# Two query tiles of an attention head handled together: one 256-column tile of probabilities, one 256-column product with the values

## The chip, the cores and the metric

The kernel runs on one core of one Trainium2 chip. The metric is the time of one execution on the device in microseconds (us): the median of 3 runs was 1680.57 us (1680.22 to 1680.72).

## The reference

Two layers work on 256 latent tokens and 256 context tokens of width 1024. Each layer is a feed-forward block, a mixer with attention heads of two kinds and a short convolution, and a second feed-forward block. In the last layer the context is only a source of keys and values. All values are float32.

```python
def gqa_attention(q, k, v):                     # heads A: 6 query heads, 2 key heads
    ...
    def block(qi):
        s = jnp.einsum('bqhgd,bkhd->bhgqk', qi, k).astype(jnp.float32) * scale
        p = jax.nn.softmax(s, axis=-1).astype(v.dtype)
        return jnp.einsum('bhgqk,bkhd->bqhgd', p, v)

def latent_mix(p, kv_ctx, cos, sin, qk_g, rpb, conv_w, rows):
    ...
    o_a = gqa_attention(qa, jnp.concatenate([ka, ka_c], axis=1), jnp.concatenate([va, va_c], axis=1))
    o_b = neighbourhood_attention(heads(qb, B_HEADS), kb, vb, kb_c, vb_c, rpb, rows)   # heads B, with a bias
    o_c = short_conv_mixer(cx, cb, cc, conv_w)
    return jnp.concatenate([o_a, o_b, o_c], axis=-1)
```

The queries and keys of heads A are normalised, multiplied by a gain (`qk_g`) and rotated; 1/8 is the scale of the scores. A latent query sees 512 keys (256 latent, 256 context), a context query sees the 256 context keys.

## The kernel before

Most products are of float32 numbers that are split into a high and a low part of type FP32R; three products (high by high, low by high, high by low) with moving operands of up to 512 columns are summed in PSUM by TensorE (`mm`, L88). `load_unit` (L95) loads a block of weights and splits it: ScalarE rounds the high part (L102), VectorE subtracts (L103).

`mixer` (L638) runs once for each layer. Tokens come in four tiles of 128 rows: 0 and 1 are latent, 2 and 3 are context. `token_block` (L656) makes V, queries and keys of heads A for a tile; it multiplies by the tile `GT` (L670), which the mixer builds first out of the gains `QK` with the factor 1/8 in it (L641 to L644). `fm_b` (L731) makes queries and keys of heads B, `fm_conv` (L756) the convolution.

`unit` (L785) handles one head and one tile of 128 queries: two products give the scores in a PSUM bank `at` (2 of them); VectorE finds the maximum (with the bias added, L796, or alone, L793); ScalarE takes the exponential with its sum (L801); VectorE divides (L803, L804); TensorE turns the probabilities over in blocks of 128 by 128 into a PSUM bank `ptr` (2 of them, L808); ScalarE copies them to an SBUF tile `PT` of up to 4 by 128 columns (L810; 3 such tiles in the first mixer, 4 in the second). Here P and PT are plain float32.

`pair` (L813) takes two heads and one query tile: two units, and then the values times the probabilities (L833 to L837) into one bank `pv`. Each of these products has 64 columns of V as its stationary operand and a block of PT as the moving one; the two heads alternate and write to partitions 0 to 63 and 64 to 127, that is, each uses one half of the array's columns. There are 4 products for 256 keys and 8 for 512 keys, and the profile shows two records for each product of plain float32. The result is copied out (L843) or, once the tiles `O` of the output projection are free, split into high and low part (`split_o`, L727).

```python
                for kb in range(nk // 128):
                    t = k0 // 128 + kb
                    for b in (1, 0):
                        vc = 64 * b if A else 128 + 64 * (2 * j + b)
                        mm(po[64 * b:64 * b + 64], V[:, t, vc:vc + 64], pts[b][:, kb], kb == 0, kb == nk // 128 - 1)
```

`attend` (L845) calls `pair` for three pairs of heads and the given query tiles: in the first mixer heads A and heads B for context and for latent queries (24 pairs), in the second one for latent queries alone (12 pairs). In the second mixer heads B of tile 0 come ahead of the convolution and those of tile 1 behind it. Behind all of this comes the output projection (L882 to L901), first all of tile 0, then all of tile 1 in the second mixer; each tile goes through `post` and `pre` (L218: a transposition at L215 and new columns of `Uh` and `Ul`) into the next feed-forward block, whose first products (`up_first`, L599) read these columns.

The order in which each engine issues its instructions is not the order of the code: a scheduler puts it together ahead of time from the code order as priority, the dependences and its own durations; the products of L837 have a raised priority. On the chip each engine then keeps to that order.

Of the kernel before, what the change touches and what calls it, by code (L numbers as in the profile page):

```python
# [25 lines left out]
def tile_hybrid_block(ctx: ExitStack, tc: tile.TileContext, xin, c2, crow, w_ada, w_ada0, bcol, gcol, win, qkg, bias_in,  # L26
# [468 lines left out]
    def ffn(ph, l, i, U, tiles, after, ada_target, mode, first=None):  # L495
# [27 lines left out]
        def up_out(fs, pss, c0, n):  # L523
            for f in fs:
# [9 lines left out]
                if f == 10:  # L534
                    n0 = len(nc.cur_bb.bb.instructions)
                    G.append(load_gate(l, mi, 1 if len(tiles) == 2 else 2))
                    if mode == "k":
                        pool.dma_start(out=ROPE, in_=rope)
                        pool.dma_start(out=CW, in_=convw)
                        pool.dma_start(out=QK.rearrange("p a d -> p (a d)"),  # L540
                                       in_=bass.AP(tensor=qkg.tensor, offset=qkg.offset, ap=[[0, 128], [1, 256]]))
                    for late in nc.cur_bb.bb.instructions[n0:]:
                        tc.add_manual_dep(late, ins.ins.name,
                                          mybir.DependencyInfo(mybir.DependencyClass.NoSync,
                                                               mybir.DependencyReason.DATA), reason="late load")
# [92 lines left out]
    def mixer(ph, l, U, after):  # L638
        full = l == 0
        order = (2, 3, 0, 1)  # L640
        GT = ph.tile([128, 8, 64], F32, name="GT", tag="GT")  # L641
        for h0, nh, row, sc in ((0, 6, 2 * l, 0.125), (6, 2, 2 * l + 1, 1.0)):
            dve.tensor_scalar(out=GT[:, h0:h0 + nh], in0=QK[:, row].unsqueeze(1).to_broadcast([128, nh, 64]),
                              scalar1=sc, scalar2=None, op0=ALU.mult)  # L644
# [11 lines left out]
        def token_block(t):  # L656
# [13 lines left out]
            dve.tensor_tensor(out=qn[:, h0:8], in0=qn[:, h0:8], in1=GT[:, h0:8], op=ALU.mult)  # L670
# [114 lines left out]
        def unit(q, k, kl, nk, bias):  # L785
# [23 lines left out]
            PT = ph.tile([128, 4, 128], F32, name="PT", tag="PT", bufs=3 if full else 4)  # L809
            act.copy(PT[:, 0:nb], pt[:, 0:nb])  # L810
            return PT

        def pair(A, j, qt):  # L813
            lat = qt < 2
            k0, nk = (0, 512) if lat else (256, 256)
            pts = []
            for b in range(2):
                qs = slice(128 * qt, 128 * qt + 128)
                ks = slice(k0, k0 + nk)
                if A:  # L820
                    pts.append(unit(AQ[:, j, b, qs], AK[:, b, ks], AL[:, b, ks], nk, None))
                else:
                    bias = None
                    if lat:
                        h = 2 * j + b
                        bias = BIAS[bn[0] % len(BIAS)]
                        bn[0] += 1
                        (sp).dma_start(out=bias[:, 0:256], in_=bias_in[l, h, qt])
                    pts.append(unit(BQ[j][b][:, qs], BK[j][b][:, ks], BL[j][b][:, ks], nk, bias))
            pb = bank("pv")  # L830
            po = pb[:, 0:128]
# [7 lines left out]
            qs = slice(128 * qt, 128 * qt + 128)  # L839
# [5 lines left out]
        def attend(A, qts):  # L845
            for j in range(3):
                for qt in qts:
                    pair(A, j, qt)

        def convert(c0, mks, n=256):  # L850
            c = slice(c0, c0 + n)
            for mk in mks:
                split_o((slice(None), mk, c), of(mk, c))
# [3 lines left out]
        if full:  # L857
            attend(True, (2, 3))
# [3 lines left out]
        attend(True, (0, 1))  # L862
        if full:
            attend(False, (2, 3))
# [3 lines left out]
            attend(False, (0, 1))  # L868
            convert(0, (0, 1, 2, 6, 7))
        else:  # L870
            attend(False, (0,))
            fm_conv()
            O.extend(new_u())
            convert(0, (0, 1, 2, 6, 7))
            convert(0, (3, 4, 5), 128)
            attend(False, (1,))
# [135 lines left out]
```

## Time and profile before

| | |
|---|---|
| median of 3 runs | 1680.57 us (1680.22 to 1680.72) |
| profiled execution | 1680.1 us, of which the traced span is 1678.2 us |
| TensorE matmul (PE) busy | 1665.8 us, 99% of the span |
| TensorE weight load (PEld) busy | 1399.2 us, 83% |
| VectorE (DVE) busy | 1134.2 us, 68% |
| ScalarE (ACT) busy | 717.5 us, 43% |
| GpSimd (POOL) busy | 47.0 us, 3% |
| granted TensorE clock, mean over the span | 0.999 of 2.4 GHz |

The first mixer runs from about 395 to 620 us of the span, the second from about 1340 to 1500 us. PE and PEld are the two halves of TensorE: a weight load can lie beside a matmul. The duration of a matmul's record is longer than the distance to the next one, since matmuls are pipelined: the time that a matmul costs is read from the distance of starts.

### The profile page before, as it was taken

What the parts mean: (1) busy time and instruction counts of PE and PEld (TensorE: products, weight loads), DVE (VectorE), ACT (ScalarE), POOL (GpSimd) and SP (SyncE); (2) the same over time, 40 slices, a digit from 0 to 9 for tenths busy, and PEclk for the clock granted to TensorE, in tenths of its full rate; (3) what the DMA queues carried; (4) which work ended last, traced back from release to release, by engine and by line L of the source; (5) the groups of instructions that cost most, each with busy time, mean ns of one, the idle gap of its engine ahead of it and who ended that gap; (6) DMA issues with size and microseconds to landing.
All of it is one profiled execution on the core that took longest, in us unless ns stands there. A gap on an engine that the chain in (4) does not pass through costs nothing.

```text
span 1678.2 us, 22858 instructions
## 1 busy us (share of the span) xinstructions
PE 1665.8 (99%) x8792; PEld 1399.2 (83%) x8792; DVE 1134.2 (68%) x1899; ACT 717.5 (43%) x1240; POOL 47.0 (3%) x77
## 2 busy tenths in 40 slices
PE   9999999999999999999999999999999999999998
PEld 7888888888877798888888888888888889879997
DVE  4578788667776665476675566787785668865554
ACT  5442222236566683322222364322223557865442
POOL 0000000001000010000000000000000010000000
PEclk9999999999999999999999999999999999999999
DMA  8476565433121234454444144665464222446552
GB/s 325 172 249 221 166 196 202 156 107 107 63 76 51 95 128 163 149 199 141 161 164 150 52 151 163 214 203 188 164 223 151 76 101 101 138 168 222 176 191 73
DMA packets 73501, 259.95 MB, mean 155 GB/s; under 512 B 8440, under 2 KB 11728, under 8 KB 72496
## 3 DMA queue, kind: packets, MB, share of 16 engines
q1 hardware_dynamic: 72144, 252.81, 44.4%
q0 software_dynamic: 1248, 5.68, 0.9%
q8 instruction: 69, 1.13, 0.3%
q14 instruction: 40, 0.33, 0.1%
HBM read 257.37 MB, written 1.09 MB: 154 GB/s over the span
## 4 chain that ended last, share of the span: by engine, by line
PE 98%; issue 1%; ACT 1%; DMA 0%; DVE 0%; SPq 0%; DVEq 0%; POOLq 0%; POOL 0%; ACTq 0%
PE mm L88 53%; PE at L88 27%; PE pv L88 14%; PE ptr L808 2%; PE ptr L215 1%; PE ptr L88 1%; DMA H<-in_xin_dram 0%; PE ptr L687 0%; PE ptr L611 0%; ACT uf L229 0%; ACT Uh L322 0%; ACT junk L198 0%; DVE w L340 0%; ACT w L336 0%; ACT w L102 0%
## 5 line engine op out<-in xcount | busy, mean ns | idle before, releaser
L88 PE MATMUL mm<-Uh,w 128*128 128x512 f32 (+1 forms) x1712 | 478.6, 358 | 0.8 <-DVE w L340 0.8
L102 ACT CAST w<-stg 128x1024 fp32r<-128x1024 f32 x254 | 266.5, 1050 | 403.6 <-PE mm L88 362.8
L103 DVE TENSOR_TENSOR w<-stg,w 128x1024 fp32r<-128x1024 f32 x254 | 310.1, 1222 | 146.1 <-ACT w L102 145.7
L88 PEld LDWEIGHTS mm<-Uh,w 128*128 128x128 f32 x1712 | 305.5, 189 | 46.8 <-DVE w L340 1.3
L152 DVE CUSTOM_DVE_ANT_0 uf<-adas,CB 128x1024 f32<-128x1024 f32 x248 | 302.9, 1221 | 18.2 <-DMA adas<-in_w_ada_dram 14.4
L88 PE MATMUL mm<-Ul,w 128*128 128x512 f32 (+1 forms) x856 | 305.9, 357 | 0.0
L88 PE MATMUL at<-Uh,w 128*128 128x512 f32 (+1 forms) x912 | 256.6, 359 | 0.1
L88 PE MATMUL mm<-w,a 128*128 128x512 f32 x924 | 223.9, 390 | 0.0
L88 PEld LDWEIGHTS mm<-w,a 128*128 128x128 f32 x924 | 172.9, 188 | 35.7
L88 PEld LDWEIGHTS at<-Uh,w 128*128 128x128 f32 x912 | 163.1, 189 | 26.6 <-issue 1.2
L88 PEld LDWEIGHTS mm<-Ul,w 128*128 128x128 f32 x856 | 161.7, 189 | 23.1
L88 PE MATMUL mm<-w,Uh 128*128 128x512 f32 (+1 forms) x544 | 170.5, 387 | 0.4 <-ACT w L102 0.4
L88 PE MATMUL at<-Ul,w 128*128 128x512 f32 (+1 forms) x456 | 163.3, 358 | 0.0
L88 PE MATMUL at<-w,a 128*128 128x512 f32 x570 | 137.3, 389 | 0.0
L88 PEld LDWEIGHTS at<-w,a 128*128 128x128 f32 x570 | 106.7, 188 | 21.9
L88 PE MATMUL pv<-Uh,w 128*128 128x512 f32 (+1 forms) x416 | 118.3, 361 | 0.3 <-DVE w L340 0.3
L88 PEld LDWEIGHTS mm<-w,Uh 128*128 128x128 f32 x544 | 100.1, 188 | 19.5 <-ACT w L102 0.7
L527 DVE TENSOR_TENSOR sg<-mm,sg 128x512 f32<-128x512 f32 (+1 forms) x80 | 50.4, 630 | 90.7 <-PE mm L88 85.1
L103 DVE TENSOR_TENSOR w<-stgx,w 128x1024 fp32r<-128x1024 f32 x58 | 71.0, 1224 | 52.6 <-ACT w L102 52.4
L88 PE MATMUL mm<-w,Ul 128*128 128x512 f32 (+1 forms) x272 | 105.1, 386 | 0.0
L88 PEld LDWEIGHTS at<-Ul,w 128*128 128x128 f32 x456 | 86.2, 189 | 12.9 <-DVE Ul L325 0.4
L526 ACT ACTIVATE sg<-at 128x512 f32<-128x512 f32 (+1 forms) x55 | 30.1, 547 | 152.6 <-PE at L88 146.1
(188 smaller groups left out, 1770.2 us busy)
## 6 DMA issues: line engine op xcount, KB each, us to landing
adas<-in_w_ada_dram SPq DMA_DIRECT2D x144, 512.0 KB, 3.7
stg<-in_wi_dram SPq DMA_DIRECT2D x122, 512.0 KB, 4.2
stg<-in_wo_dram SPq DMA_DIRECT2D x66, 512.0 KB, 3.3
stg<-in_win_dram SPq DMA_DIRECT2D x40, 512.0 KB, 3.2
stgx<-in_wi_dram SPq DMA_DIRECT2D x38, 512.0 KB, 4.3
stgx<-in_wo_dram SPq DMA_DIRECT2D x22, 512.0 KB, 4.3
stg<-in_woa_dram SPq DMA_DIRECT2D x16, 512.0 KB, 3.2
stg<-in_wi_tm_dram SPq DMA_DIRECT2D x16, 512.0 KB, 3.2
```

The costliest lines, as they stand in the source:

```text
L88: pe.matmul(out, lhsT=lhsT, rhs=rhs, start=first, stop=last)
L102: act.copy(w[:, 0], s)
L103: dve.tensor_tensor(out=w[:, 1], in0=s, in1=w[:, 0].bitcast(F32), op=ALU.subtract)
L152: dve.tensor_tensor_reduce(out=junk, in0=s, in1=CB[:, v], op0=ALU.mult, op1=ALU.add, scale=1.0, scalar=0.0, accum_out=ada_mc[m][:, v, cb:c ...
L215: pe.transpose(pt[:, b], xn[:, 128 * k:128 * k + 128], I)
L526: act.activation(sg[:, 0:n], pss[f, 0][:, 0:n], AF.Silu)
L527: dve.tensor_tensor(out=sg[:, 0:n], in0=pss[f, 1][:, 0:n], in1=sg[:, 0:n], op=ALU.mult)
L808: pe.transpose(pt[:, b], P[:, 128 * b:128 * b + 128], I)
```

## The change

Probabilities of both query tiles of a head go into one tile PT of 4 by 256 columns, each unit filling its 128 columns; `pair` now takes two heads and two query tiles (four units, head 1 first), and each product with the values moves 256 columns. PT has 2 buffers in both mixers. In the second mixer the convolution moves behind the first pair of heads B, and both query tiles of the other two pairs come behind it. Beside this, `GT` is gone: 1/8 is multiplied into `QK` once, behind its load in the first feed-forward block, and the product with the gains becomes two instructions (queries, keys).

```diff
                         pool.dma_start(out=QK.rearrange("p a d -> p (a d)"),
                                        in_=bass.AP(tensor=qkg.tensor, offset=qkg.offset, ap=[[0, 128], [1, 256]]))
+                        qk = QK.rearrange("p (l a) d -> p l a d", a=2)[:, :, 0]
+                        dve.tensor_scalar(out=qk, in0=qk, scalar1=0.125, scalar2=None, op0=ALU.mult)
...
-        GT = ph.tile([128, 8, 64], F32, name="GT", tag="GT")
-        for h0, nh, row, sc in ((0, 6, 2 * l, 0.125), (6, 2, 2 * l + 1, 1.0)):
-            dve.tensor_scalar(out=GT[:, h0:h0 + nh], in0=QK[:, row].unsqueeze(1).to_broadcast([128, nh, 64]),
-                              scalar1=sc, scalar2=None, op0=ALU.mult)
...
-            dve.tensor_tensor(out=qn[:, h0:8], in0=qn[:, h0:8], in1=GT[:, h0:8], op=ALU.mult)
+            for ha, hb, row in ((h0, 6, 2 * l), (6, 8, 2 * l + 1)):
+                if ha < hb:
+                    dve.tensor_tensor(out=qn[:, ha:hb], in0=qn[:, ha:hb],
+                                      in1=QK[:, row].unsqueeze(1).to_broadcast([128, hb - ha, 64]), op=ALU.mult)
...
-        def unit(q, k, kl, nk, bias):
+        def unit(q, k, kl, nk, bias, PT, c):
...
-            PT = ph.tile([128, 4, 128], F32, name="PT", tag="PT", bufs=3 if full else 4)
-            act.copy(PT[:, 0:nb], pt[:, 0:nb])
-            return PT
-
-        def pair(A, j, qt):
-            lat = qt < 2
+            act.copy(PT[:, 0:nb, c:c + 128], pt[:, 0:nb])
+
+        def pair(A, j, q0):
+            lat = q0 == 0
             k0, nk = (0, 512) if lat else (256, 256)
...
+            pts = [None, None]
+            for b in (1, 0):
+                pts[b] = ph.tile([128, 4, 256], F32, name="PT", tag="PT", bufs=2)
+                for qi in range(2):
+                    qt = q0 + qi
+                    qs = slice(128 * qt, 128 * qt + 128)
+                    if A:
+                        unit(AQ[:, j, b, qs], AK[:, b, ks], AL[:, b, ks], nk, None, pts[b], 128 * qi)
...
             pb = bank("pv")
-            po = pb[:, 0:128]
+            po = pb[:, 0:256]
...
-            qs = slice(128 * qt, 128 * qt + 128)
+            qs = slice(128 * q0, 128 * q0 + 256)
...
-            attend(False, (0,))
+            attend(False, 0, (0,))
             fm_conv()
             O.extend(new_u())
-            convert(0, (0, 1, 2, 6, 7))
-            convert(0, (3, 4, 5), 128)
-            attend(False, (1,))
+            convert(0, (0, 1, 2, 3, 6, 7))
+            attend(False, 0, (1, 2))
```

The scheduler's order moves with it. **TensorE, second mixer, the last two pairs of heads.** `pv<-PT,V` are the products with the values (64 columns of V by 128 or 256 columns of PT), `ptr<-I,P` the turned probabilities, `mm<-w,Uh` and `mm<-w,Ul` the output projection. Before:

```order
L88 MATMUL pv<-PT,V 64x128 x8
L808 MATMUL ptr<-I,P 128x128 x4
L88 MATMUL mm<-w,Uh 128x512
L88 MATMUL mm<-w,Ul 128x512
L88 MATMUL mm<-w,Uh 128x512 x2
L88 MATMUL mm<-w,Ul 128x512
L88 MATMUL mm<-w,Uh 128x512 x2
L88 MATMUL mm<-w,Ul 128x512
L88 MATMUL mm<-w,Uh 128x512 x2
L88 MATMUL mm<-w,Ul 128x512
L88 MATMUL mm<-w,Uh 128x512 x3
L88 MATMUL pv<-PT,V 64x128 x8
```

And with the change:

```order
L88 MATMUL pv<-PT,V 64x256 x7
L809 MATMUL ptr<-I,P 128x128 x8
L88 MATMUL mm<-w,Uh 128x512 x3
L809 MATMUL ptr<-I,P 128x128 x4
L88 MATMUL pv<-PT,V 64x256
L88 MATMUL mm<-w,Ul 128x512
L88 MATMUL mm<-w,Uh 128x512
L88 MATMUL mm<-w,Ul 128x512
L88 MATMUL mm<-w,Uh 128x512
L88 MATMUL mm<-w,Ul 128x512
```

Before, the products of a pair stood together, 4 or 8 in a row, in all 36 pairs. Now the first product (head 1, first key block) stands alone as soon as the tile of head 1 is whole, and the other 3 or 7 follow later, behind other work; this is so in all 18 pairs.

**TensorE, second mixer, behind the last product with the values.** `ptr<-I,xn` is the transposition of token tile 0 (L215), `at<-w,Uh` the first product of the next feed-forward block that reads the new columns of tile 0. Before:

```order
L88 MATMUL pv<-PT,V 64x128 x8
L88 MATMUL mm<-w,Ul 128x512
L88 MATMUL mm<-w,Uh 128x512
L88 MATMUL mm<-w,Ul 128x512
L88 MATMUL mm<-w,Uh 128x512
L215 MATMUL ptr<-I,xn 128x128 x8
L88 MATMUL mm<-w,Uh 128x512 x2
L88 MATMUL mm<-w,Ul 128x512
L88 MATMUL mm<-w,Uh 128x512 x2
```

And with the change:

```order
L88 MATMUL mm<-w,Uh 128x512 x2
L88 MATMUL mm<-w,Ul 128x512
L88 MATMUL mm<-w,Uh 128x512
L215 MATMUL ptr<-I,xn 128x128 x8
L88 MATMUL at<-w,Uh 128x512
L88 MATMUL mm<-w,Uh 128x512
L88 MATMUL at<-w,Ul 128x512
```

Before, 18 products of the output projection of tile 1 stood between that transposition and the first `at<-w,Uh`; now there are none. Behind the last product with the values stand 51 products of the output projection in place of 22.

**VectorE, first feed-forward block, the new product on `QK`** (L543 is the added line):

```order
L103 TENSOR_TENSOR w<-stg,w 128x1024
L543 TENSOR_SCALAR QK<-QK 128x2x64
L152 ISA uf,mc<-adas,CB 128x1024
L152 ISA mc 128x1
L527 TENSOR_TENSOR sg<-mm,sg 128x512
```

Before, the same rows stood without L543.

## Rows read from the trace of the kernel before

**Rows 1.** The page, part 4: the chain that ended last, share of the span by engine.
```profile
PE 98%; issue 1%; ACT 1%; DMA 0%; DVE 0%; SPq 0%; DVEq 0%; POOLq 0%; POOL 0%; ACTq 0%
```

**Rows 2.** Windows, mixers: from:to, length, busy PE, PEld, DVE, ACT, POOL; clock; DMA.
```profile
395.00:620.00 225.00, 224.09 (x1328) 182.72 (x1328) 156.62 (x363) 145.49 (x339) 14.49 (x18) 1.00 0.24 81
536.00:560.00 24.00, 23.52 (x177) 17.80 (x176) 19.11 (x66) 18.42 (x59) 0.00 (x0) 1.00 0.24 78
1340.00:1500.00 160.00, 158.74 (x1021) 134.32 (x1021) 121.94 (x270) 113.90 (x234) 11.02 (x17) 1.00 0.35 120
```

**Rows 3.** Tile V: all products with the values (ns min/median/max, first and last start).
```profile
L88 PE MATMUL pv<-PT,V x480: 272/273/324, 450.8 to 1476.1; 128*64 128x128 f32 x160
```

**Rows 4.** Timeline of PE round one block (start us, us, engine, line, what, count).
```profile
450.46 0.40 PE L88 MATMUL mm<-Ul,w 128*128 128x512 f32 x1
450.79 0.66 PE L88 MATMUL pv<-PT,V 128*64 128x128 f32 x8
451.38 0.44 PE L808 MATMUL ptr<-I,P 128*128 128x128 f32 x2
```

**Rows 5.** Timeline of PE round a block of 512 keys, second mixer.
```profile
1439.66 0.40 PE L88 MATMUL mm<-w,Uh 128*128 128x512 f32 x1
1439.98 1.09 PE L88 MATMUL pv<-PT,V 128*64 128x128 f32 x16
1441.01 0.96 PE L88 MATMUL at<-w 128*128 128x512 f32 x3
```

**Rows 6.** The chain in order of time: start us, us, what.
```profile
64.40 5.44 PE at L88 x24
```

**Rows 7.** Groups by line and form, 8 to 600 us: xcount | busy us, mean ns.
```profile
L88 PE MATMUL ptr<-adas,S 128*32 128x128 f32 x256 | 8.6, 276 | 0.0
L88 PE MATMUL at<-AL,AQ 128*128 128x512 f32 x12 | 4.7, 393 | 0.0
L88 PE MATMUL at<-AL,AQ 128*128 128x256 f32 x12 | 3.5, 288 | 0.0
```

**Rows 8.** Tile ptr, 49 to 57 us: float32 products of 4 columns (ns min/median/max).
```profile
L88 PE MATMUL ptr<-SELM,R x4: 168/210/253, 50.9 to 56.5; 128*128 128x4 f32 x4
```

**Rows 9.** Groups of weight loads by form, whole span.
```profile
L88 PEld LDWEIGHTS pv<-PT,V 128*64 128x64 f32 x480 | 25.5, 136 | 10.9 <-issue 5.5 <-ACT P L801 2.0 <-ACT PT L810 1.1
L88 PEld LDWEIGHTS ptr<-adas,S 128*32 128x32 f32 x256 | 6.5, 109 | 2.4 <-issue 2.1
```

**Rows 10.** Timeline, second mixer's end: token tile 0 into the next block.
```profile
1477.29 1.04 PE L215 MATMUL ptr<-I,xn 128*128 128x128 f32 x8
...
1478.08 0.70 PE L88 MATMUL mm<-w,Uh 128*128 128x512 f32 x2
...
1479.81 1.05 ACT L102 CAST w<-stg 128x1024 fp32r<-128x1024 f32 x1
...
1480.76 0.62 ACT L233 CAST Uh<-uf 128x512 fp32r<-128x512 f32 x1
...
1482.29 0.39 PE L88 MATMUL at<-w,Uh 128*128 128x512 f32 x1
```

**Rows 11.** Timeline of PE: token tile 1 into the next block.
```profile
1495.55 0.50 PE L88 MATMUL at<-w,Uh 128*128 128x512 f32 x1 [1.11 <-ACT Uh L233]
```

**Rows 12.** Groups by form, first mixer: copies of turned probabilities out of PSUM.
```profile
L810 ACT COPY PT<-ptr 128x512 f32<-128x512 f32 x24 | 13.7, 587 | 7.8 <-PE ptr L808 7.8
```

**Rows 13.** Tile GT: its four instructions and its readers (ns min/median/max).
```profile
L670 DVE TENSOR_TENSOR qn<-qn,GT x8: 286/684/693, 409.0 to 1384.4; 128x512 f32<-128x512 f32 x6, 128x128 f32<-128x128 f32 x2
L643 DVE TENSOR_SCALAR GT<-QK x4: 217/287/352, 402.7 to 1349.3; 128x384 f32<-128x384 f32 x2, 128x128 f32<-128x128 f32 x2
```

**Rows 14.** Tile QK: its load.
```profile
L540 POOL DMA_DIRECT2D QK<-in_qkg_dram x1: 536/536/536, 122.2 to 122.2; - x1
...
DMA to landing us min/median/max: 8.1/8.1/8.1
```

**Rows 15.** Timeline of DVE, first feed-forward block.
```profile
137.66 1.22 DVE L103 TENSOR_TENSOR w<-stg,w 128x1024 fp32r<-128x1024 f32 x1
```

More of the change, by code (lines that the diff above doesn't have):

```diff
@@ L808, in unit @@
                 pe.transpose(pt[:, b], P[:, 128 * b:128 * b + 128], I)
-            PT = ph.tile([128, 4, 128], F32, name="PT", tag="PT", bufs=3 if full else 4)
-            act.copy(PT[:, 0:nb], pt[:, 0:nb])
-            return PT
-        def pair(A, j, qt):
-            lat = qt < 2
-            k0, nk = (0, 512) if lat else (256, 256)
-            pts = []
-            for b in range(2):
-                qs = slice(128 * qt, 128 * qt + 128)
[L819 to L829, printed above, removed]
+            act.copy(PT[:, 0:nb, c:c + 128], pt[:, 0:nb])
+        def pair(A, j, q0):
+            lat = q0 == 0
+            k0, nk = (0, 512) if lat else (256, 256)
+            ks = slice(k0, k0 + nk)
+            pts = [None, None]
[6 more added lines that the diff above has]
+                        unit(AQ[:, j, b, qs], AK[:, b, ks], AL[:, b, ks], nk, None, pts[b], 128 * qi)
+                    else:
+                        bias = None
+                        if lat:
+                            h = 2 * j + b
+                            bias = BIAS[bn[0] % len(BIAS)]
+                            bn[0] += 1
+                            (sp).dma_start(out=bias[:, 0:256], in_=bias_in[l, h, qt])
+                        unit(BQ[j][b][:, qs], BK[j][b][:, ks], BL[j][b][:, ks], nk, bias, pts[b], 128 * qi)
             pb = bank("pv")
-            po = pb[:, 0:128]
+            po = pb[:, 0:256]
             with tc.high_priority():
@@ L838, in pair @@
             mk = j if A else 3 + j
-            qs = slice(128 * qt, 128 * qt + 128)
+            qs = slice(128 * q0, 128 * q0 + 256)
             if O:
@@ L843, in pair, with attend @@
                 act.copy(of(mk, qs), po)
[L845 to L848, printed above, removed]
+        def attend(A, q0, js=(0, 1, 2)):
+            for j in js:
+                pair(A, j, q0)
         def convert(c0, mks, n=256):
@@ L857, in mixer @@
         if full:
-            attend(True, (2, 3))
+            attend(True, 2)
         for t in (0, 1):
@@ L861, in mixer @@
         fm_b()
-        attend(True, (0, 1))
+        attend(True, 0)
         if full:
-            attend(False, (2, 3))
+            attend(False, 2)
             fm_conv()
@@ L867, in mixer @@
             convert(256, range(8))
-            attend(False, (0, 1))
+            attend(False, 0)
             convert(0, (0, 1, 2, 6, 7))
         else:
-            attend(False, (0,))
+            attend(False, 0, (0,))
             fm_conv()
             O.extend(new_u())
-            convert(0, (0, 1, 2, 6, 7))
-            convert(0, (3, 4, 5), 128)
-            attend(False, (1,))
+            convert(0, (0, 1, 2, 3, 6, 7))
+            attend(False, 0, (1, 2))
             act.activation(work.tile([128, 1024], BF16, name="junk", tag="junk")[:, 0:1], last_sm[0], AF.Silu)
```

## The prediction

> **What bounds the kernel now.** I read the chain that ended last first: 98% of the span is TensorE [rows 1]. Then the busy time by stretch: in the first mixer TensorE is busy for 224.09 of 225 us, in the second for 158.74 of 160, while VectorE and ScalarE are busy for some 65 to 76% [rows 2]. So inside the mixers too the kernel costs what TensorE's instructions cost, and a microsecond more or less there is one in the end. The granted clock is at its upper level (2.4 GHz) in both stretches, and nothing in the change empties TensorE for long; I leave the clock alone. What the other engines do counts only where TensorE comes to wait.
>
> **The products with the values, before.** There are 480 records with 128 moving columns [rows 3]: 12 pairs with 256 keys (8 records each) and 24 with 512 keys (16 records). What a block costs I read from starts. A product of 512 columns comes every 0.227 us (24 in 5.44 us) [rows 6]. In the first example the last such product starts at 450.46, so the next one could start at 450.69; behind the block of 8 TensorE starts on something else at 451.38 [rows 4]: 0.69 us. With 512 keys: 1439.66 plus 0.23 is 1439.89, then 1441.01 [rows 5]: 1.12 us for 16 records. The 8 records more cost 0.43 us. The two heads use different halves of the columns and go side by side, so this is four steps of two records, 0.108 us a step; and 0.69 less four steps leaves **0.26 us that a block costs whatever its length**, in front of it and behind it. All of it: 12 x 0.69 + 24 x 1.12 = 35.2 us.
>
> **The same, with the change.** First the step of 256 columns, which no row shows. A float32 record of 4 columns takes 168 ns at the least [rows 8], one of 128 columns 272 [rows 3]: 0.84 ns a column. FP32R records go from 288 to 393 ns between 256 and 512 columns [rows 7]: 0.41 ns a column. So float32 pays by the column, at twice the rate of FP32R, and 128 columns at 0.84 ns are 0.107 us, which is the whole step. I take 2 x 0.108 = 0.216 us. Bounds: below, 0.108 (columns free), above, 0.227, the step of an FP32R record of twice as many columns. Moving 256 columns at once then saves nothing by itself: half the steps at twice the price. What could be saved is the 0.26 us of each block: 36 blocks would become 18, 4.7 us.
>
> But the new order does not keep the blocks whole. In all 18 pairs the first product stands alone and the other 3 or 7 stand further on. That keeps 36 blocks, so the 4.7 us are not saved. And the lone product uses half the array: its two records cost 2 x 0.216 = 0.43 us with nobody beside them. In the rest head 0 has one product more than head 1 (2 to 1 or 4 to 3), so it takes as many steps as the whole block would have taken: 4 or 8. Sum: 18 x (0.43 + 0.26) + 6 x (4 x 0.216 + 0.26) + 12 x (8 x 0.216 + 0.26) = 12.4 + 6.7 + 23.9 = 43.0 us. **The values cost 7.8 us more than before**, which is 18 x 0.43.
>
> **What of it lies beside waiting.** TensorE's idle time in the mixers is 0.9 and 1.3 us [rows 2]; 0.48 of it lies in 536 to 560 us, where heads B of the context run with the least other work. There longer products fill gaps: -0.5 us. Bounds: 0 and -1.1 (that, and half of the rest). The other 1.1 us of the second mixer is one wait, next.
>
> **The end of the second mixer.** Before, tile 0 of the tokens was through its attention early; between its transposition and the first product on its new columns stood 18 products, and nothing waited long. Now both tiles end together, and no product stands there. From the first other instruction behind the transposition (1478.08) to the end of the rounding of the first half of the new columns (1480.76 + 0.62 = 1481.38) are 3.3 us [rows 10], with one rounding of weights of 1.05 us between. Without it, 2.25 us. I take 2.8 us of new waiting, bounds 2.25 and 4.2 (until 1482.29, when the first product did start). Against that, tile 1 before waited 1.11 us for its columns [rows 11]; now 20 products (4.5 us) stand in front of that product, longer than the 3.3 us, and the wait goes. Together +1.7 us, bounds +1.1 and +3.1.
>
> **At no cost.** `GT` goes (4 instructions of 0.22 to 0.35 us), and the product with the gains splits: two instructions of at most 0.69 and 0.29 us for one of 0.69 [rows 13], at most 6 x 0.29 us more on VectorE, which is busy for 157 of 225 us in the first mixer and has TensorE's other products as cover; without that cover, 0.3 us for each of four latent or context tiles. The new product on `QK` needs its load, landed at 122.2 + 8.1 = 130.3 us [rows 14]; it stands behind a weight split that starts at 137.66 [rows 15], so it waits for nothing and delays VectorE by some 0.2 us. Copies of results become half as many and twice as wide: ScalarE gains a little that nobody waits for. SP issues the same loads in nearly the same order; POOL's order is unchanged.
>
> **The new dependence.** Two PT tiles serve four units, so the first copy of a pair waits for the last product of the pair before. Only two `ptr` banks hold turned probabilities meanwhile, so the third transposition waits for that copy: 0.59 us [rows 12], against 0.40 us of the second transposition in front of it (half of the 0.79 us between 1477.29 and 1478.08 for eight blocks [rows 10]). If nothing else stands between, that is 0.19 us a pair, and with the way of the signals I put 0.3 us (an estimate): 5.4 us in all. The order puts other products between in most places; I take 0 and keep 5.4 as the bound.
>
> **Sum.** 7.8 - 0.5 + 1.7 = +9.0 us on the profiled execution's 1680.1: **1689.1 us**. The median of the runs is 0.5 us above that execution, less than any term here.
>
> **The rivals.**
> *Columns are nearly free* (faster). If the step of a record is set by its weight load and not by its columns, 256 columns also cost 0.108 us. Steps: 240 before; now 18 x 2 + 6 x 4 + 12 x 8 = 156. That is 84 x 0.108 = 9.1 us less, and 1680.1 - 9.1 - 0.5 + 1.7 = 1672.2 us. It decides from a step under 0.166 us on (240 x 0.108 / 156). For it: each record here has a load of its own, of 136 ns [rows 9], longer than the step. Against it: float32 records with loads of 32 columns (109 ns) [rows 9] take 276 ns [rows 7], those with 64 columns 273 [rows 3]: the shorter load buys nothing; and the record of 4 columns is short. The Trainium skill speaks for this rival, in the page "TensorE: Matmul & The Clock Gate", section "Back-to-back issue gap": sustained, about 81 ns at 128 columns and 131 ns at 512, far less than in proportion. By that ratio a step of 256 columns would be about 1.2 times one of 128 (an estimate from that page), and the sum would come to about 1676 us. The trace does not agree: 512 columns come every 227 ns here.
>
> *Lone products without the fixed part* (no change to slightly slower). The 0.26 us was read from blocks with both halves at work. If a lone product slips in without it, 18 x 0.26 = 4.7 us are off: 1684.4 us, and with the bounds of the two waiting terms (-1.1, +1.1) 1683.2. For it: no row shows a lone block. Against it: the part in front and behind looks the same for 8 and 16 records.
>
> *PT starves TensorE* (slower still): the bound above, 1689.1 + 5.4 = 1694.5 us. For it: in 536 to 560 us ScalarE is busy for 18.42 of 24 us, VectorE for 19.11 [rows 2]. Against it: the scheduler knows of the two tiles and has put products in between.
>
> **How the numbers follow.** Forecast 0.62, lone products without the fixed part 0.14, starving 0.16, columns nearly free 0.08. A measurement can tell 0.2%, 3.4 us, from no change: under 1677.2 is faster, over 1683.9 slower. The forecast with its bounds (1687.9 from 7.8 - 1.1 + 1.1, 1691.0 from 7.8 + 0 + 3.1, and 1692.8 with steps of 0.227, which make the 7.8 into 9.6) is slower; the second rival falls on both sides of 1683.9, and I give it to "same"; the first is faster. Faster 0.08, same 0.14, slower 0.78. The range of 8 in 10 is 1683 to 1695: it leaves out the fast rival, the least of the second one and what lies beyond starving.
>
> **What would show it.** Right: 240 records of 128*64 by 256 columns at about 0.216 us from start to start, each lone pair of them with some 0.7 us between its neighbours; TensorE still busy for nearly the whole of both mixers, which are longer by 7 to 8 us together before the end of the second one; a wait of TensorE of 2 to 3 us for the new columns of tile 0 behind the transposition at L215. Wrong: records of 256 columns that follow at under 0.17 us; lone products with no gap round them; or waits of TensorE for copies to PT, which would be listed under its waits in the mixers.

## The result and the profile after

The changed kernel takes **1697.97 us** (median of 4 runs, 1697.57 to 1698.64) against 1680.52 for the kernel before: a ratio of 1.0104, 95% interval 1.0092 to 1.0116. That is 17.4 us slower. The direction was forecast; the size, +9.0 us, was not, and the time lies above the range of 1683 to 1695. The profiled execution has a span of 1695.6 us, 17.4 longer than before, so the traces can be compared term by term.

The page of after, part 4, the chain that ended last, by engine (before: [rows 1]):

```profile
PE 96%; ACT 1%; DVE 1%; DMA 1%; issue 1%; SPq 0%; POOL 0%; DVEq 0%; POOLq 0%; ACTq 0%
```

Windows of after; columns as in [rows 2]. The first mixer is nearly as full as it was (1.62 us idle of 225, before 0.91). The second one, which is longer, has 7.17 us idle of 180, where before it was 1.26 of 160. Three quarters of that (3.54 and 1.82) lie in the last two windows, and there the granted clock is no longer 1.00:

```profile
395.00:620.00 225.00, 223.38 (x1133) 173.30 (x1132) 151.83 (x354) 140.15 (x316) 14.49 (x17) 1.00 0.22 76
1340.00:1520.00 180.00, 172.83 (x970) 140.75 (x969) 128.90 (x279) 119.82 (x238) 11.55 (x18) 0.98 0.34 116
...
1492.00:1497.00 5.00, 1.46 (x10) 0.86 (x8) 3.30 (x8) 4.88 (x11) 0.53 (x1) 0.94 0.50 159
1497.00:1503.20 6.20, 4.38 (x10) 3.01 (x11) 5.61 (x8) 4.76 (x9) 1.11 (x3) 0.50 0.73 262
```

Tile V of after, the products with the values (ns min/median/max, first and last start; before: [rows 3]):

```profile
L88 PE MATMUL pv<-PT,V x240: 379/379/431, 450.7 to 1479.7; 128*64 128x256 f32 x120
```

There are half as many records, and they are 106 ns longer (median). Timeline of PE of after, a lone product and a whole block of 7 in the first mixer (start us, us, engine, line, what, count; before: [rows 4, 5]):

```profile
590.70 0.86 PE L88 MATMUL mm<-w,Uh 128*128 128x512 f32 x3
591.49 0.65 PE L88 MATMUL pv<-PT,V 128*64 128x256 f32 x2
592.06 0.50 PE L88 MATMUL mm<-w,Ul 128*128 128x512 f32 x1
...
596.73 0.39 PE L88 MATMUL mm<-w,Uh 128*128 128x512 f32 x1
597.05 1.94 PE L88 MATMUL pv<-PT,V 128*64 128x256 f32 x14
598.92 0.50 PE L88 MATMUL mm<-w,Uh 128*128 128x512 f32 x1
```

Read as the prediction read them: behind three products of 0.227 us the next could start at 591.38; TensorE goes on at 592.06, so the lone product costs 0.68 us. The block of 7 runs from 596.96 to 598.92, 1.96 us. That is 8 steps of 0.216 us, as the prediction counts them, and 0.23 of fixed part.

The end of the second mixer, timeline of after on PE, with the rows of ACT and DVE that stand ahead of the new columns (in brackets: idle time before, and what ended it; before: [rows 10, 11]):

```profile
1474.24 0.66 PE L809 MATMUL ptr<-I,P 128*128 128x128 f32 x4 [1.18 <-ACT PT L810]
...
1492.56 1.09 PE L215 MATMUL ptr<-I,xn 128*128 128x128 f32 x8 [0.20 <-ACT xn L210]
1492.63 1.04 ACT L102 CAST w<-stg 128x1024 fp32r<-128x1024 f32 x1
1493.58 0.59 ACT L198 ACTIVATE junk<-mm 128x512 bf16<-128x512 f32 x1
...
1494.16 1.50 ACT L229 ACTIVATE uf<-ptr,COLS,GP 128x128 f32<-128x128 f32 x4
...
1495.53 1.06 ACT L102 CAST w<-stg 128x1024 fp32r<-128x1024 f32 x1
...
1496.46 1.17 ACT L233 CAST Uh<-uf 128x512 fp32r<-128x512 f32 x2
1496.84 1.22 DVE L103 TENSOR_TENSOR w<-stg,w 128x1024 fp32r<-128x1024 f32 x1
1497.16 0.79 PE L88 MATMUL at<-w,Uh 128*128 128x512 f32 x1 [3.50 <-ACT Uh L233]
1497.75 0.63 PE L88 MATMUL mm<-w,Uh 128*128 128x512 f32 x1
1497.97 1.41 DVE L480 SCALAR_TENSOR_TENSOR H<-yg,rr,H 128x512 f32<-128x512 f32 x2
...
1499.30 1.28 DVE L234 TENSOR_TENSOR Ul<-uf,Uh 128x512 fp32r<-128x512 f32 x2
...
1500.04 0.80 PE L88 MATMUL at<-w,Ul 128*128 128x512 f32 x1 [1.66 <-DVE Ul L234]
...
1500.63 1.06 PE L88 MATMUL at<-w,Uh 128*128 128x512 f32 x2
...
1501.48 0.63 PE L88 MATMUL at<-w,Ul 128*128 128x512 f32 x1
...
1503.19 0.65 PE L88 MATMUL at<-w,Uh 128*128 128x512 f32 x2
```

In the kernel before, the statistic of tile 1 started only behind the rounding of the first half of Uh, timeline of before on ACT:

```profile
1481.29 0.59 ACT L198 ACTIVATE junk<-mm 128x512 bf16<-128x512 f32 x1
```

TensorE waits twice in the changed kernel: for the high part Uh of tile 0's new columns, and, two products later, for the low part Ul. Ahead of Uh, ScalarE has a statistic of tile 1 (L198) and two roundings of weights (L102); ahead of Ul, VectorE has a split of weights and the update of H of tile 1. Then the products come about 0.43 us apart (1500.63, two of them, 1501.48) instead of 0.227.

**Where the 17.4 us are.** From the starts of all TensorE records I added up two things, in the same way for each kernel: what all blocks with the values cost (from the point where the instruction ahead lets the next one start to the start of the second instruction behind, less the step of the first one), and the waits over 0.1 us between all other instructions (start against that same point, with steps of 0.227 us for 512 columns, 0.114 for 256 and 0.109 for a transposition of 128).

| us | before | after | difference |
|---|---|---|---|
| blocks with the values, first mixer | 23.23 | 28.67 | +5.4 |
| blocks with the values, second mixer | 14.34 | 17.39 | +3.1 |
| waits, first mixer | 1.93 | 3.03 | +1.1 |
| waits, second mixer and its end | 2.55 | 10.32 | +7.8 |
| sum | | | +17.4 |

The blocks hold some 0.1 us more each than in the prediction, which stopped at the first instruction behind; by its count they cost 35.2 us before and 43.7 after.

The last row holds 3.67 us in front of 1497.16 and 2.06 in front of 1500.04 (the profile's brackets start later), 0.36 in front of the transposition, 1.9 by which the ten products from 1497.16 to 1503.19 are further apart than at full clock, 1.3 at 1474.24 and smaller ones; of before's 2.55, the wait of 1.4 for tile 1's columns is gone. The question for the experiments: are these terms what they seem, and what makes the waits?

### The profile page after: what moved, and what is told of

It is laid out like the page before. It is cut to its first block, busy times and chain, and to the rows that moved or that the text cites. A ratio compares the mean times of both kernels' runs of the same rounds, so it can differ in the third digit from the quotient of the medians.

```text
span 1695.6 us, 22363 instructions
## 1 busy us (share of the span) xinstructions
PE 1675.4 (99%) x8552; PEld 1394.1 (82%) x8552; DVE 1133.2 (67%) x1896; ACT 714.7 (42%) x1220; POOL 50.6 (3%) x77
## 4 chain that ended last, share of the span: by engine, by line
PE 96%; ACT 1%; DVE 1%; DMA 1%; issue 1%; SPq 0%; POOL 0%; DVEq 0%; POOLq 0%; ACTq 0%
PE mm L88 52%; PE at L88 27%; PE pv L88 14%; PE ptr L809 1%; PE ptr L215 1%; PE ptr L88 1%; DMA stg<-in_wi_tm_dram 0%; DMA H<-in_xin_dram 0%; DVE w L103 0%; ACT w L102 0%; ACT P L802 0%; PE ptr L688 0%; PE ptr L613 0%; DVE H L480 0%; ACT PT L810 0%
## 5 line engine op out<-in xcount | busy, mean ns | idle before, releaser
L102 ACT CAST w<-stg 128x1024 fp32r<-128x1024 f32 x254 | 266.5, 1050 | 417.5 <-PE mm L88 365.3
```

The lines of the kernel that those rows point to most:

```text
L102: act.copy(w[:, 0], s)
```

## The experiments

Theory: the new order costs the 8.5 us of lone products, and tile 0, which now arrives with tile 1, leaves nothing for TensorE to do while its columns are made. Rivals: 256 columns are dear by themselves; two PT tiles starve TensorE; the order, not the late attention, makes the waits. In the diffs `-` and `+` stand against the kernel named.

| kernel | median us (runs) | ratio to before, 95% interval | blocks, first + second mixer | waits, first + second |
|---|---|---|---|---|
| e1_whole_blocks | 1687.29 (1687.07 to 1687.81) | 1.0039, 1.0023 to 1.0054 | 19.31 + 12.85 | 6.52 + 11.62 |
| e2_second_mixer_as_before | 1686.24 (1686.14 to 1686.63) | 1.0033, 1.0021 to 1.0045 | 28.66 + 14.34 | 2.63 + 2.88 |
| e3_first_mixer_whole | 1680.15 (1679.75 to 1680.94) | 0.9998, 0.9989 to 1.0006 | 19.31 + 14.34 | 5.85 + 2.60 |
| e4_gains_alone | 1680.73 (1680.44 to 1681.41) | 1.0001, 0.9992 to 1.0011 | as before | 2.05 + 2.54 |
| e5_four_tiles_first_mixer | 1677.45 (1676.92 to 1678.76) | 0.9984, 0.9975 to 0.9992 | 19.31 + 14.34 | 4.06 + 2.83 |
| e6_three_pt_second_mixer | 1697.28 (1697.17 to 1697.94) | 1.0100, 1.0087 to 1.0114 | as after | 2.62 + 10.79 |
| e7_filled_wait | 1696.00 (1695.77 to 1696.19) | 1.0092, 1.0078 to 1.0106 | as after | 2.63 + 1.9, and 6.4 of added work |
| e8_heads_b_by_tile | 1684.00 (1683.63 to 1685.94) | 1.0023, 1.0013 to 1.0034 | 19.31 + 13.38 | 6.40 + 7.01 |
| e9_low_half_on_gpsimd | 1697.15 (1696.34 to 1698.10) | 1.0099, 1.0082 to 1.0116 | as after | 2.62 + 10.33 |
| e10_turn_earlier | 1680.89 (1680.38 to 1681.54) | 1.0002, 0.9993 to 1.0011 | 19.31 + 13.37 | 6.16 + 4.30 |
| e11_all_together | 1678.90 (1678.43 to 1679.52) | 0.9991, 0.9982 to 1.0000 | 19.31 + 13.37 | 4.33 + 4.49 |

**e1_whole_blocks**, against the changed kernel: head 0, whose tile is ready last, goes first, so no product can slip ahead of the block.

```diff
-                    for b in (1, 0):
+                    for b in (0, 1):
                         vc = 64 * b if A else 128 + 64 * (2 * j + b)
                         mm(po[64 * b:64 * b + 64], V[:, t, vc:vc + 64], pts[b][:, kb], ...)
```

> The changed kernel with one edit: the products with the values begin with head 0, whose tile is filled last, so that no product can be placed ahead of the others (the new order has 18 blocks of 4 or 8 in place of 36). Theory: the lone products cost the changed kernel their own two steps (0.43 us) and one more block's fixed part (0.30 us) each, so 18 x 0.73 = 13.1 us come back and the median is about 1685; what stays above the kernel before is the end of the second mixer. Rival (the two PT tiles starve TensorE, and it matters little how the products stand): the copies wait as long as before, the median stays above 1692.

Measured: 10.7 us faster than the changed kernel (9.6 between the profiled executions), 2.3 less than the theory gave. The blocks cost 32.2 us instead of 46.1, and 5.4 less than the 37.6 of before: so 256 columns at once do pay once the blocks are whole, by what stands round 18 blocks (by the prediction's count it is 4.1 us, where it had 4.7). But the waits grow by 4.8 us, 3.5 of it in the first mixer, and the sum stays above the kernel before.

**e2_second_mixer_as_before**, against the changed kernel: the second mixer's attention by query tile and in the order of before (128 columns, four PT tiles of 128); the first mixer keeps its lone products.

```diff
-        attend(True, 0)
+        if full:
+            attend(True, 0)
+        else:
+            attend_tile(True, (0, 1))
...
-            attend(False, 0, (0,))
+            attend_tile(False, (0,))
...
-            convert(0, (0, 1, 2, 3, 6, 7))
-            attend(False, 0, (1, 2))
+            convert(0, (0, 1, 2, 6, 7))
+            convert(0, (3, 4, 5), 128)
+            attend_tile(False, (1,))
```

> The changed kernel with the second mixer's attention as it was before (query tiles apart, 128 columns, tile 0 of heads B ahead of the convolution); the first mixer as changed, lone products included. Theory: the end of the second mixer costs some 7 us (waits for the columns of token tile 0, half clock, less the wait of before), its lone products and waits for copies some 4 to 5 us more, so the median falls by 11 to 12 us to about 1686. Rival (the loss goes with the number of pairs alone, 12 in the first mixer and 6 in the second): a third of 17.4 us comes back, 1692.

Measured: 1686.24, as the theory had it. The second mixer's change is worth 11.7 of the 17.4 us, the first mixer's the other 5.7, nearly all of it lone products (+5.4).

**e3_first_mixer_whole**: both edits together, so that the first mixer has whole blocks of 256 columns and the second one is as before.

> Both edits: blocks kept whole in the first mixer, second mixer's attention as before. Theory: the first mixer then has 12 blocks in place of 24 and pays the fixed part of 0.30 us 12 times less, 3.6 us under the kernel before: about 1677. Rival (256 columns or the two PT tiles cost something of their own): no faster than the kernel before, 1680 or more.

Measured: 1680.15, no gain: the rival. The blocks give 3.9 us back and the first mixer's waits take 3.9. Waits of e3_first_mixer_whole between 530 and 560 us (engine, line, waited for: us in total, times, longest):

```profile
ACT PT L810 <- PE pv L88: 3.8, 2, 2.9
...
PE at L88 <- ACT P L802: 1.4, 2, 0.8
```

ScalarE's copies to PT wait for the block that reads the tile. That block is whole now, so both tiles come free only at its end; the exponentials behind the copy are late, and TensorE waits for them.

**e4_gains_alone**: the kernel before with only the change to `GT` and `QK`.

> The kernel before with only the edit of the gains (the factor 1/8 multiplied into QK once, the tile GT gone, the product with the gains in two instructions). Theory: within 0.5 us of the kernel before, 1680.5, since TensorE has other products meanwhile. Rival (the longer chain of VectorE in front of the transposition at L687 holds TensorE up): 1 to 3 us slower.

Measured: 1680.73. This edit costs nothing that can be told.

**e5_four_tiles_first_mixer**, against e3_first_mixer_whole: every second pair of heads A and of the context's heads B in the first mixer puts its probabilities in the gate tile, which is idle there.

```diff
+            pn[0] += 1
+            GP2 = None
+            if pn[0] % 2 == 0 and not O:
+                GP2 = work.tile([128, 2, 1024], F32, name="G", tag="G").rearrange("p b (k c) -> p b k c", c=256)
             for b in (1, 0):
-                pts[b] = ph.tile([128, 4, 256], F32, name="PT", tag="PT", bufs=2)
+                pts[b] = GP2[:, b] if GP2 is not None else ph.tile([128, 4, 256], F32, name="PT", tag="PT", bufs=2)
```

> This is e3_first_mixer_whole (whole blocks of 256 columns in the first mixer, the second mixer's attention as before), with four PT tiles in place of two in the first mixer's heads A and the context's heads B (the other two lie in the gate tile, which is idle there). In e3_first_mixer_whole TensorE waited for 5.9 us in the first mixer (before 1.9), 3.9 us more than before, and the trace put that at 534 to 557 us, with copies to PT that waited for products. Theory (two PT tiles cause that): those copies no longer wait, TensorE's waits in the first mixer fall to about 2 us, and the time is about 1676.5 us, 3.9 below the kernel before. Rival (ScalarE and VectorE can't prepare the probabilities any faster there, with however many tiles): the waits stay between 5 and 6 us and the time near 1680.

Measured: 2.7 us faster than e3_first_mixer_whole and 2.9 faster than the kernel before, the fastest of these kernels. The profiled executions are only 1.5 us apart, and the waits explain no more than that (6.9 us where there were 8.5). The copies' wait for products is gone from the same stretch, but the waits of the first mixer fell to 4.1 us, not to 2. What is left there, waits of e5_four_tiles_first_mixer between 530 and 560 us:

```profile
PE at L88 <- DVE nmx L797: 1.1, 1, 1.1
PE at L88 <- ACT P L802: 0.9, 2, 0.6
```

So the theory holds for about half of the 3.9 us. The list puts the rest down to the rival, ScalarE's and VectorE's own pace in a stretch where heads B of the context have little other work beside them; no run changed that pace.

**e6_three_pt_second_mixer**, against the changed kernel (one bias tile fewer makes the room):

```diff
-        BIAS = [... for x in range(2 if full else 4)]
+        BIAS = [... for x in range(2 if full else 3)]
...
-                pts[b] = ph.tile([128, 4, 256], F32, name="PT", tag="PT", bufs=2)
+                pts[b] = ph.tile([128, 4, 256], F32, name="PT", tag="PT", bufs=2 if full else 3)
```

> The changed kernel with three PT tiles instead of two in the second mixer (three bias tiles instead of four make the room). Theory (of the loss over the forecast, only the waits for copies to PT, 1.4 us at 1474 and 0.4 at 1454, come from the number of PT tiles; the rest is the wait for tile 0's new columns and what follows it): 1 to 2 us off, 1696 to 1697 us. Rival (starving by PT is what the forecast missed): the 8.4 us above the forecast go, 1690 us or less.

Measured: 0.7 us less, with ranges that overlap, so the theory's 1 to 2 us are not shown either. Timeline of PE of e6_three_pt_second_mixer:

```profile
1473.32 0.96 PE L88 MATMUL mm<-w,Uh 128*128 128x512 f32 x3 [0.59 <-ACT Uh L729]
...
1496.11 0.50 PE L88 MATMUL at<-w,Uh 128*128 128x512 f32 x1 [3.70 <-ACT Uh L233]
...
1498.99 0.79 PE L88 MATMUL at<-w,Ul 128*128 128x512 f32 x1 [2.15 <-DVE Ul L234]
```

The wait for a copy at 1474 is gone; a shorter one for other columns stands there, and TensorE waits somewhat longer at the end (the changed kernel has 3.5 and 1.7). The rival is out: starving by PT is not what the forecast missed in the second mixer.

**e7_filled_wait**, against the changed kernel:

```diff
         for hb, pt in normed_t(t):
+            if (l, j, t, hb) == (1, 2, 0, 1):
...
+                p = bank("pv")
+                for _ in range(28):
+                    ins = pe.matmul(p, lhsT=keep_on["w"][:, 0:128], rhs=keep_on["w"], start=True, stop=True)
...
```

> The changed kernel with 28 more products of 512 columns right behind the transposition of token tile 0 in the second mixer, whose sum nobody reads: TensorE is busy for 6.4 us (28 x 0.227) where it now waits for the new columns of that tile, and the rest of the order is unchanged. Theory (part of the loss there is the granted clock, which fell to 0.50 behind the wait and made the next products come every 0.43 us): the clock stays near 1.00 from 1492 to 1503 us, the products behind come every 0.227 us, and the time falls by about 1.3 us to 1696.6, though there is more work. Rival (the low clock costs nothing, since the products wait for the columns anyway): the added products end after the columns are there, and the time stays or grows by up to 2.6 us (6.4 less the 3.8 of the first wait), 1698 to 1700.6.

Measured: 2.0 us faster with 6.4 us more work. Timeline of PE of e7_filled_wait:

```profile
1492.41 1.09 PE L215 MATMUL ptr<-I,xn 128*128 128x128 f32 x8 [0.21 <-ACT xn L210]
1493.26 6.63 PE L231 MATMUL pv<-WK 128*128 128x512 f32 x28
1499.72 0.39 PE L88 MATMUL at<-w,Uh 128*128 128x512 f32 x1
...
1500.41 0.62 PE L88 MATMUL at<-w,Uh 128*128 128x512 f32 x2
1500.87 0.39 PE L88 MATMUL at<-w,Ul 128*128 128x512 f32 x1
...
1501.78 0.62 PE L88 MATMUL at<-w,Uh 128*128 128x512 f32 x2
```

Windows of e7_filled_wait:

```profile
1492.00:1497.00 5.00, 4.79 (x25) 3.94 (x25) 3.35 (x8) 4.79 (x11) 0.55 (x1) 1.00 0.57 180
1497.00:1503.20 6.20, 6.20 (x29) 5.12 (x28) 5.62 (x8) 4.77 (x9) 1.09 (x2) 1.00 0.69 254
```

The clock stays at 1.00 and the products come 0.23 us apart. From the transposition's start to the tenth product behind it are 9.37 us (1501.78 less 1492.41), in the changed kernel 10.63 (1503.19 less 1492.56): 1.26 us for the clock, as expected. The rest of the 2.0 us was not settled. The profiled executions are 1.5 us apart, and this stretch holds most of it. The wait for a copy to PT at 1474 is some 0.9 us shorter here, with the same order of instructions there, but the first product with the values starts more than a microsecond later than in the changed kernel. In e9_low_half_on_gpsimd, too, that wait is 0.6 us shorter.

**e8_heads_b_by_tile**, against e1_whole_blocks: heads B of the second mixer by query tile, as before, with both heads in one PT tile; heads A stay 256 wide.

```diff
-            attend(False, 0, (0,))
+            for j in range(3):
+                pair_tile(j, 0)
             fm_conv()
             O.extend(new_u())
-            convert(0, (0, 1, 2, 3, 6, 7))
-            attend(False, 0, (1, 2))
+            convert(0, (0, 1, 2, 6, 7))
+            convert(0, (3, 4, 5), 128)
+            for j in range(3):
+                pair_tile(j, 1)
```

> e1_whole_blocks (whole blocks of 256 columns) with heads B of the second mixer by query tile as in the kernel before: tile 0 ahead of the convolution, tile 1 behind it, both heads side by side in one PT tile; heads A stay 256 columns wide. The schedule still has no product of another kind between the transposition of token tile 0 and the first product on its columns. Theory (the end's loss is the schedule's: what stands behind the transposition, not how late the attention of tile 0 is): TensorE still waits 3 to 4 us behind the transposition, the time falls by some 3 to 5 us against e1_whole_blocks (1687.3), to 1682 to 1684. Rival (lateness of tile 0's attention): the wait behind the transposition goes, 1679 us or less.

Measured: 1684.00. Tile 0's attention is early again, and still TensorE waits behind its transposition. Timeline of e8_heads_b_by_tile, ACT and PE:

```profile
1476.87 1.15 ACT L210 ACTIVATE xn<-H,rr 128x1024 f32<-128x1024 f32 x1 [1.05 <-POOL rr L108]
...
1480.56 1.04 PE L215 MATMUL ptr<-I,xn 128*128 128x128 f32 x8
...
1483.94 0.50 PE L88 MATMUL at<-w,Uh 128*128 128x512 f32 x1 [2.34 <-ACT Uh L233]
...
1486.49 0.79 PE L88 MATMUL at<-w,Ul 128*128 128x512 f32 x1 [1.82 <-DVE Ul L234]
1487.08 1.05 PE L88 MATMUL at<-w,Uh 128*128 128x512 f32 x2
```

The rows were normalised by 1478.02; the transposition was queued behind 11 products and started 2.5 us later, with none left to put behind it. The theory held: two waits, 4.2 us together where it had 3 to 4, and a time at the upper end of what it gave. The clock falls here too, in a window of the same kernel:

```profile
1484.00:1489.60 5.60, 3.78 (x9) 2.72 (x10) 5.43 (x9) 3.75 (x7) 0.09 (x1) 0.70 0.96 339
```

**e10_turn_earlier**, against e8_heads_b_by_tile: an order-only dependence puts the last 12 products of tile 1's output projection behind that transposition.

```diff
+                if turned and (t, hf) == (1, 1) and k >= 4:
+                    for x in nc.cur_bb.bb.instructions[-3:]:
+                        tc.add_manual_dep(x, turned[0], ..., reason="behind")
```

> e8_heads_b_by_tile with one edit in the order: the last 12 products of the output projection of tile 1 stand behind the transposition of token tile 0 instead of ahead of it. In e8_heads_b_by_tile (1684.0) that tile's normalised rows were ready at 1478.0 us and its transposition came only at 1480.6, behind 11 products, and then TensorE waited 2.3 us for Uh and 1.8 us for Ul, with the granted clock at 0.70 behind it. Theory (the order is what costs there): both waits shrink to under 1 us together, the clock stays at 1.00, TensorE's waits of the second mixer fall from 7.0 to about 3 us, and the time is about 1680, no more than the kernel before. Rival (what is put behind the transposition is missing in front of tile 1's columns a little later, so the wait only moves): 1682.5 us or more.

Measured: 1680.89, 3.1 us faster, level with the kernel before. Timeline of PE of e10_turn_earlier (`mm` stands on L89 there):

```profile
1477.84 1.04 PE L216 MATMUL ptr<-I,xn 128*128 128x128 f32 x8
...
1482.15 0.50 PE L89 MATMUL at<-w,Uh 128*128 128x512 f32 x1 [0.51 <-ACT Uh L239]
...
1483.59 0.50 PE L89 MATMUL at<-w,Ul 128*128 128x512 f32 x1 [0.70 <-DVE Ul L240]
1483.92 0.63 PE L89 MATMUL at<-w,Uh 128*128 128x512 f32 x2
...
1496.11 0.50 PE L89 MATMUL at<-w,Uh 128*128 128x512 f32 x1 [0.89 <-ACT Uh L239]
```

The two waits are 1.2 us by the profile instead of 4.2 (the theory had under 1), and the products behind follow 0.23 us apart. The waits of the second mixer are 4.3 us where the theory had 3: it was right on most of it, and the rival on 0.9 us, which TensorE now waits for tile 1's columns. In this kernel the order did it. In the changed kernel the transposition itself waited for its rows (0.20 us at 1492.56), so products moved from in front of it to behind it should only move the wait; this is argued, no run tried it.

**e9_low_half_on_gpsimd**, against the changed kernel:

```diff
-            dve.tensor_tensor(out=U[1][:, ks, c], in0=uf[:, ks], in1=U[0][:, ks, c].bitcast(F32), op=ALU.subtract)
+            (pool if (l, j, t) == (1, 2, 0) else dve).tensor_tensor(out=U[1][:, ks, c], ...)
```

> The changed kernel with one edit: the subtraction that makes the low part Ul of token tile 0 behind the second mixer (L234, two instructions of 128x512) runs on GpSimd, which is idle there, instead of VectorE, where a product with the gate, a split of weights and two updates of H of tile 1 (0.68, 1.22 and 1.41 us) stand ahead of it. Theory (TensorE's second wait, 2.2 us until Ul at 1500.0, is VectorE's queue and not the work on Ul itself): Ul is there about a microsecond behind Uh, the second wait falls to 1 us or less, the first one (4.1 us, for Uh) stays, and the time falls by 1 to 2 us, to 1696 to 1697. Rival (Ul is late because the whole chain of tile 0 is late, or GpSimd takes as long for it as VectorE's queue did): the second wait stays near 2 us or grows, and the time is 1697.5 us or more.

Measured: 0.8 us less, with ranges that overlap: inconclusive on the time, but the trace answers. Timeline of e9_low_half_on_gpsimd:

```profile
1496.22 3.69 POOL L234 TENSOR_TENSOR Ul<-uf,Uh 128x512 fp32r<-128x512 f32 x2 [0.16 <-ACT Uh L233]
1497.01 3.45 DVE L480 SCALAR_TENSOR_TENSOR H<-yg,rr,H 128x512 f32<-128x512 f32 x2
...
1498.27 0.80 PE L88 MATMUL at<-w,Ul 128*128 128x512 f32 x1 [1.35 <-POOL Ul L234]
```

GpSimd started at once behind Uh, where VectorE in the changed kernel came to it 2.2 us behind the first half (1499.30 against 1496.46 + 0.59); but it took 1.85 us for each half. The second wait shrinks by 0.3 us only, and from the transposition to the tenth product are 10.06 us, 0.6 less; the next two still came at half clock. VectorE's queue does delay Ul; GpSimd, beside VectorE's work, is too slow to profit from that.

**e11_all_together**: e10_turn_earlier with the four tiles of e5_four_tiles_first_mixer.

> e10_turn_earlier with the four PT tiles of e5_four_tiles_first_mixer in the first mixer. If the two edits don't touch each other, the first mixer gives the same 2.7 us as between e3_first_mixer_whole (1680.15) and e5_four_tiles_first_mixer (1677.45), and the second mixer's heads A in blocks of 256 columns save 1.0 us of products against e5_four_tiles_first_mixer: about 1677, 0.5 us less than e5_four_tiles_first_mixer. Rival (heads A of 256 columns make waits in the second mixer that eat the 1.0 us): 1678 to 1679.

Measured: 1678.90, the rival. Heads A in blocks of 256 columns give 1.0 us of products in the second mixer, and its waits are 1.7 us longer than in e5_four_tiles_first_mixer.

## Why the prediction was wrong

**Right: the products with the values.** The step is 0.216 us, the lone product 0.68 us where 0.69 stood, the extra cost 8.5 us where 7.8 stood; e1_whole_blocks shows that it is the lone products (whole blocks are 5.4 us cheaper than before, not dearer; 4.1 by the prediction's count, near its 4.7). Both rivals on the values, columns that are nearly free and lone products without the fixed part, are out. So is any cost of `GT` and `QK` (e4_gains_alone).

**Wrong, and the step that failed: the end of the second mixer, "+1.7 us, bounds +1.1 and +3.1".** It measured +6.6: 8.0 us of waits and slow products, less the old wait of 1.4 for tile 1's columns, which did go, as it said. Three parts of it:

- The wait for the high part was 3.67 us, where 2.8 was taken and 4.2 was the upper bound. The bound was sound, the choice was not: the rounding of weights that it counted by half (1495.53) was still there, and the statistic at 1493.58, which before ran behind the first half of Uh, now stood ahead of all of this.
- The low part was forgotten. The sum's chain ended with the first half of Uh; the third product behind the transposition needs Ul. Before, 18 products gave that time as well. It cost 2.06 us.
- The clock: "nothing in the change empties TensorE for long; I leave the clock alone". The waits emptied it. The ten products lost 1.9 us, most of it at half clock; with the wait filled, e7_filled_wait got 1.26 back. In e8_heads_b_by_tile waits of 2.3 and 1.8 us were enough for the clock to fall; whether the prediction's own 2.8 us alone would have been, no run shows.

**Wrong in sign: "longer products fill gaps: -0.5 us".** The first mixer's waits grew by 1.1 us (by 0.7 in the four later kernels with the same first mixer). Its bound of -1.1 was also added up wrongly: that is 0.48 us and all of the rest, where it says half.

**Taken at 0, with the right bound: the new dependence.** "I take 0 and keep 5.4 as the bound." In the second mixer it and smaller waits cost some 1.2 us (mainly at 1474.24). In the first mixer the changed kernel shows 1.1 us more of waits, and with whole blocks it is the 3.9 us of e3_first_mixer_whole, of which four tiles bring back about half. That the lone products fill the time of these waits in the changed kernel is argued from the two runs, not shown by itself.

The misses add up: 0.7 for the values, 1.6 in the first mixer, 4.9 at the end, 1.2 for copies and the rest: 8.4 us, which is 17.4 less 9.0. The top of the range joined the forecast with the starving alone, but taking all the waiting terms at their upper bounds (0, 3.1 and 5.4 us, on 7.8) would have given only 1696.4, still less than was measured. The range failed because the end cost 6.6 us, over twice its own bound.

**Still open:** why the scheduler puts the transposition of tile 0 last in e8_heads_b_by_tile, where heads A are 256 columns wide and both heads of a pair of heads B share one PT tile; the runs show only that it does and what it costs.

## What to carry to other kernels

In this kernel wider moving operands of plain float32 save only a block's fixed part, and only if the block stays whole: look in the order for products that slip out of it, and count the buffers that a whole block holds until its end. Where a change lets two tiles finish together, count the products left behind the first one's transposition; if there are none, price the whole way to the last operand that the next products read, low part and queued work of the other engines included, and then the clock.

## What the runs showed of the hardware that was not expected

- **The granted clock fell for a wait of a few microseconds.** TensorE was busy for 1.46 us of the 5 before 1497; in the 6.2 us behind, the granted clock was 0.50 (1.2 GHz), and products of 512 columns came 0.43 us apart; from 1503.2 on they came 0.23 apart again. With the wait filled it stayed at 1.00. It also stayed there behind shorter waits: 1.1 us in the kernel before, 0.5 and 0.7 us in e10_turn_earlier.
- **VectorE was slowed by GpSimd.** In e9_low_half_on_gpsimd the two updates of H on VectorE took 3.45 us beside GpSimd's two subtractions of 3.69 us; in the changed kernel, with GpSimd idle, they took 1.41. The Trainium skill ("SBUF — State Buffer", section "SBUF: two separate sides") says that a GpSimd instruction that reads SBUF and a VectorE instruction with two inputs in SBUF, as this update has, hold a shared pair of ports in turn, for a whole instruction. The trace agrees with that as far as one run can show it. Whether GpSimd was slowed as well, no run shows, since none has its subtraction alone.
- **A lone product pays the fixed part in full.** It costs 0.68 us, two steps of 0.216 us and 0.25 us round them; a block of 14 records has 0.23 us round it.
